# Opening feed-forwards and embedding gates with two tile pairs, chunk by chunk

## The chip, the cores and the metric

The kernel runs on one core of one Trainium2 chip. The metric is the device time of one execution in microseconds (us). Three runs of the kernel before took 1033.48, 1034.87 and 1036.57 us; their median, 1034.87, is the time before. In one more execution the hardware profiler took down every instruction.

## The reference

The program is a trunk of two layers over 256 positions of 1024 features. All weights and activations are float32.

```
for i in range(DEPTH):                                   # DEPTH = 2
    x = x + 0.5 * swiglu(rms_norm(x, norm_ffn1[i]), w_ffn1_gu[i], w_ffn1_down[i])
    h = rms_norm(x, norm_mix[i])
    mix = stick_breaking_attention(...) if i % 2 == 0 else multiscale_pool_mixer(...)
    x = x + mix
    x = x + 0.5 * swiglu(rms_norm(x, norm_ffn2[i]), w_ffn2_gu[i], w_ffn2_down[i])
    gate = sigmoid(rms_norm(x, norm_ple[i]) @ w_ple_gate[i])
    x = x + gate * (p[i] @ w_ple_proj[i])
```

`swiglu(h)` is `(silu(h @ w_gate) * (h @ w_up)) @ w_down` with an inner width of 2816. `rms_norm` divides by the root of the mean square over the 1024 features and multiplies by a gain.

## The kernel before, in words

**Layout.** x is held transposed: eight chunks of 128 features, each a tile of 128 partitions by 256 positions (`x[:, d]`). Every matmul multiplies a 128x128 tile of weights by a chunk, and sums over the chunks in a PSUM bank. A bank holds 512 columns, so two results of 256. Results rotate over six banks, three of the tag `z` and three of the tag `mm` (`next_bank`); two more, `st` and `o`, serve the statistics and attention.

**Splitting.** For accuracy each operand is split into a high part (rounded to the matmul's format) and a low part (the rest), and each product is three matmuls: high by high, high by low, low by high (`mm3`, lines 202 to 206; the matmul itself is line 130).

**Weights.** They come in 163 units of 128x2048 values, 16 tiles each, in the order of use. SyncE issues their loads. `divide` (lines 158 to 181) makes the high part (line 179 on ScalarE, or line 177 on VectorE) and the low part (line 181 on VectorE or GpSimd), in pieces. The table `SPLIT` gives for a unit (number of pieces, highs on VectorE, lows on GpSimd); the lows on GpSimd are the last ones. Units that aren't in it have (2, 0, 0). Raw values, highs and lows have three buffers each, so a unit's split can be written when the third unit before it is no longer read. `unit(u)` loads up to u + 3 and splits u and u + 1; `ahead` splits two units past the newest.

**Norm.** The gain goes into the chunks at once: line 268 makes the high part of a chunk on ScalarE, line 269 the low part on VectorE (tiles `xx`). The squares are made on the engine that `SQUARE` names (p GpSimd, a ScalarE, v VectorE, lines 280 to 282) and added up on GpSimd (line 283; the first square is line 273, the last sum is on VectorE). `statistics` (lines 293 to 326) adds them over the partitions with two matmuls into the bank `st` and makes r, the reciprocal root, with two ScalarE operations and four on VectorE (lines 288 to 291). r multiplies results after their matmuls, so matmuls needn't wait for it.

**Stages.** A feed-forward (`ffn`) has 22 tile pairs, one unit each, gate and up in one bank. Then 11 units for the way down: eight chunks of 22 tiles, each added to x (lines 400 to 403) and handed to the next norm at once. `project_late` begins a stage: the first unit takes the early chunks for both its results, and then the last ones (`LATE_FFN` says how many). `LEAD` says after how many pairs the statistics stand in TensorE's order; results wait in their banks till then. The embedding gate (`embed`) has four units and gives each result of 256 columns a bank of its own: lines 776 to 779 multiply by r, take the sigmoid (ScalarE), multiply by the projection and add to x, by way of a tile in SBUF, and then the next norm begins on that chunk. After the last layer the chunks are stored instead, and the last one goes in two halves.

**Units around the joints.** 49 is the embedding projection of layer 0, and 50 to 82 its second feed-forward (50 to 71 pairs, 72 to 82 the way down). 83 to 86 are the gates of layer 0. 87 to 119 are the first feed-forward of layer 1, 120 its embedding projection, 121 to 125 pooling. 126 to 158 are its second feed-forward, and 159 to 162 its gates.

**Order.** TensorE's and SyncE's instructions run in the order in which the program writes them (`manual_schedule`). A planner orders the other engines' when the program is built: what is ready goes first, by priority. `high_priority` blocks go ahead of the rest; otherwise what was written earlier goes first. Gates of the embedding, with the norm behind them, have high priority; splits and the feed-forwards' gates haven't. Engines wait for each other by semaphores that the planner places; two engines' accesses to one PSUM bank are kept apart by it.

Of the kernel before, what the change touches and what calls it, by code (L numbers as in the profile page):

```python
# [11 lines left out]
F32 = mybir.dt.float32  # L12
F32R = mybir.dt.float32r
AF = mybir.ActivationFunctionType
ALU = mybir.AluOpType

P = 128
D = 1024
S = 256
# [37 lines left out]

LATE_FFN = (1, 1, 2, 2)  # L60
LEAD = (2, 1, 2, 2)

# [3 lines left out]
    ("ffn1", 0): "aavvavpv",  # L66
    ("mixer", 0): "ppppapvp",
    ("ffn2", 0): "apppvavv",
    ("ple", 0): "paappppa",
    ("ffn1", 1): "ppvvpppv",  # L70
    ("mixer", 1): "aapppapp",
    ("ffn2", 1): "ppppapvv",
# [25 lines left out]
def trunk(ctx: ExitStack, tc: tile.TileContext, gxT, pT, wts, outT):  # L98
# [17 lines left out]
    def name(s):  # L116
        uid[0] += 1
        return f"{s}_{uid[0]}"
# [6 lines left out]
    def next_bank():  # L125
        turn[0] += 1
        return bank("z" if turn[0] % 2 else "mm")
# [65 lines left out]
    def ahead():  # L193

        divide(newest[0] + 2)
# [63 lines left out]
    def begin_norm():  # L259
        nonlocal xx, xh, xl, acc  # L260
        xx = act.tile([P, 2, NC, S], F32R, tag="xx", bufs=2, name=name("xx"))
        xh, xl = xx[:, 0], xx[:, 1]
        acc = tmp.tile([P, S], F32, tag="acc", name=name("acc"))
# [67 lines left out]
    def project(u, out, src, order=range(NC), halves=(0, 1), start=None, stop=None):  # L331

        start = order[0] if start is None else start
        stop = order[-1] if stop is None else stop
        two = isinstance(out, list)
        for i in halves:
            dst = out[i][:, :S] if two else out[:, i * S : (i + 1) * S]
            for k in order:
                mm3(
                    dst, tile_of(u, i * 8 + k), (src[0][:, k], src[1][:, k]),  # L340
                    (two or i == 0) and k == start, k == stop,
                )

    def project_late(u, out, src, order, late):

        a, b = order[: NC - late], order[NC - late :]
        project(u, out, src, a, start=order[0], stop=order[-1])
        project(u, out, src, b, start=order[0], stop=order[-1])


    def ffn(n, u0, order, last_norm, aside=None, before=None):
        late, lead = LATE_FFN[n], LEAD[n]
        with tc.tile_pool(name=name("ffn"), bufs=1) as pool:
            hx = pool.tile([P, 2, NFF, S], F32R, name=name("hx"))
            hh, hl = hx[:, 0], hx[:, 1]

            def gated(j, ps):
                s = tmp.tile([P, S], F32, tag="s", name=name("s"))
                nc.vector.tensor_mul(s, ps[:, :S], r)  # L359
                nc.scalar.activation(s, s, AF.Silu)  # L360
                nc.vector.tensor_mul(s, s, ps[:, S:])
                nc.scalar.activation(hh[:, j], s, AF.Copy)
                nc.vector.tensor_sub(hl[:, j], s, f(hh[:, j]))

            waiting = []
            for j in range(NFF):
                ps = next_bank()
                if u0 + j == 0:
                    for k in range(NC):
                        for i in range(2):  # L370
                            mm3(
                                ps[:, i * S : (i + 1) * S], tile_of(0, 2 * k + i),
                                (xh[:, k], xl[:, k]), i + k == 0, k == NC - 1,
                            )
                elif j == 0:
                    project_late(u0, ps, (xh, xl), order, late)
                else:
                    project(u0 + j, ps, (xh, xl))
                waiting.append((j, ps))
                if j == lead - 1:  # L380
                    if before is not None:
                        before()
                    statistics()
                if j >= lead - 1:
                    for w in waiting:
                        gated(*w)
                    waiting = []
                ahead()
                if j == 4 and aside is not None:
                    aside()  # L390
            r_ffn = r
            begin_norm()
            for d in range(NC):
                ps = next_bank()
                for k in range(NFF):
                    w = tile_of(u0 + NFF, d * NFF + k)
                    mm3(ps[:, :S], w, (hh[:, k], hl[:, k]), k == 0, k == NFF - 1)
                t = tmp.tile([P, S], F32, tag="s", name=name("s"))
                with tc.high_priority():
                    nc.vector.scalar_tensor_tensor(  # L400
                        out=t, in0=ps[:, :S], scalar=0.5, in1=r_ffn, op0=ALU.mult, op1=ALU.mult
                    )
                    nc.vector.tensor_add(x[:, d], x[:, d], t)  # L403
                    last_norm(d, d == 0)
        return u0 + UNITS_FFN
# [350 lines left out]
        return proj, some  # L756

    def embed(u0, proj, after):
        xs = (xh, xl)
        for i in range(4):  # L760
            banks = [next_bank(), next_bank()]
            if i == 0:
                project_late(u0, banks, xs, list(range(NC)), 1)
                statistics()
                if after is not None:
                    begin_norm()
            else:
                project(u0 + i, banks, xs)
            for half in range(2):
                d = 2 * i + half  # L770
                t = tmp.tile([P, S], F32, tag="s", name=name("gate"))
                with tc.high_priority():
                    src = banks[half][:, :S]
                    n = S // 2 if after is None and d == NC - 1 else S
                    for c in (slice(i, i + n) for i in range(0, S, n)):
                        nc.vector.tensor_mul(t[:, c], src[:, c], r[:, c])
                        nc.scalar.activation(t[:, c], t[:, c], AF.Sigmoid)
                        nc.vector.tensor_mul(t[:, c], t[:, c], proj[:, d, c])  # L778
                        nc.vector.tensor_add(x[:, d, c], x[:, d, c], t[:, c])  # L779
                    if after is not None:  # L780
                        after(d, d == 0)
                if after is None:
                    nc.sync.dma_start(outT[:, d], x[:, d])
            ahead()
        return u0 + 4


# [142 lines left out]
```

## Time and profile before

| | |
|---|---|
| median of three runs | 1034.87 us (1033.48 to 1036.57) |
| the profiled execution | 1035.21 us, its span 1033.5 |
| TensorE (PE) busy | 985.5 us, 7942 matmuls, mean granted clock 0.975 |
| VectorE (DVE) busy | 708.4 us |
| ScalarE (ACT) busy | 532.1 us |
| GpSimd (POOL) busy | 297.2 us |

A row of the timeline gives start, duration, engine, line, operation, tiles written and read, and in brackets how long the engine was idle before and what ended it. A row of a group gives the count, the busy time, the mean of one in ns, and the idle time ahead with what ended it. A row of stretches gives for each engine the busy time and, in brackets, the instructions, then the granted clock of TensorE, the DMA share and GB/s. A row of waits gives the total, how many and the longest. A row of the chain gives start and duration of a piece of the chain that ended last.

### The profile page before, as it was taken

How to read it: one execution, taken by the hardware profiler on the slowest of the kernel's cores; microseconds unless marked ns; L12 is line 12 of the kernel's file. 1: busy time of each engine (PE TensorE's matmuls, PEld its weight loads, DVE VectorE, ACT ScalarE, POOL GpSimd, SP SyncE). 2: the span in 40 equal slices, each digit the busy share in tenths (PEclk: the TensorE clock that was granted, in tenths of full speed). 3: DMA queues.
4: the chain of work that ended last, by engine and by line, in shares of the span. 5: the costliest groups of instructions: out<-in, count | busy, mean ns of one | idle time of the engine just before them, and what ended most of it. 6: DMA issues, size and time to landing. Idle time of an engine off the chain costs nothing.

```text
span 1033.5 us, 19057 instructions
## 1 busy us (share of the span) xinstructions
PE 985.5 (95%) x7942; PEld 967.8 (94%) x7942; DVE 708.4 (69%) x1021; ACT 532.1 (51%) x875; POOL 297.2 (29%) x294
## 2 busy tenths in 40 slices
PE   8999999998788899999999799999998799999998
PEld 8999999987787899999999799999988699999997
DVE  7865655588998855665668776565568966565666
ACT  5654444557686655454446455444352565454443
POOL 4300003746574540000166510000256510000253
PEclk8999999998898999999999899999999899999999
DMA  7655454453221265455553455545443265555541
GB/s 246 258 201 183 185 200 168 164 175 151 82 82 42 87 241 204 167 201 181 190 194 130 163 189 188 191 177 205 166 161 123 94 235 201 176 192 196 174 161 42
DMA packets 26727, 174.81 MB, mean 169 GB/s; under 512 B 2960, under 2 KB 4496, under 8 KB 6032
## 3 DMA queue, kind: packets, MB, share of 16 engines
q1 hardware_dynamic: 26640, 173.59, 46.7%
q8 instruction: 62, 1.02, 0.4%
q14 instruction: 25, 0.20, 0.1%
HBM read 172.53 MB, written 1.05 MB: 168 GB/s over the span
## 4 chain that ended last, share of the span: by engine, by line
PE 82%; DVE 14%; ACT 2%; issue 1%; DMA 1%; SPq 0%; DVEq 0%; ACTq 0%
PE mm L130 41%; PE z L130 40%; DVE s L676 2%; DVE xx L269 2%; DVE wl L181 2%; DVE ql L510 1%; PE o L130 1%; DMA gx<-gxT 1%; DVE kl L506 1%; DVE gx L779 1%; DVE sql L442 0%; DVE gate L778 0%; DVE sph L435 0%; DVE qkt L488 0%; DVE sp L532 0%
## 5 line engine op out<-in xcount | busy, mean ns | idle before, releaser
L179 ACT ACTIVATE wh<-raw 128x1024 fp32r<-128x1024 f32 (+2 forms) x408 | 342.0, 867 | 296.5 <-PE mm L130 114.3
L181 DVE TENSOR_TENSOR wl<-raw,wh 128x1024 fp32r<-128x1024 f32 (+2 forms) x299 | 333.1, 1129 | 96.1 <-ACT wh L179 95.6
L130 PE MATMUL mm<-xx,wh 128*128 128x256 f32 x1856 | 335.5, 282 | 0.0
L130 PE MATMUL z<-xx,wh 128*128 128x256 f32 x1600 | 293.3, 284 | 10.9 <-DVE xx L269 7.4
L130 PEld LDWEIGHTS mm<-xx,wh 128*128 128x128 f32 x1856 | 287.5, 190 | 0.5
L130 PEld LDWEIGHTS z<-xx,wh 128*128 128x128 f32 x1600 | 249.5, 191 | 13.3 <-DVE xx L269 9.3
L130 PE MATMUL mm<-xx,wl 128*128 128x256 f32 x928 | 261.4, 282 | 0.1
L130 PE MATMUL z<-xx,wl 128*128 128x256 f32 x800 | 226.3, 283 | 1.9 <-DVE wl L181 1.9
L181 POOL TENSOR_TENSOR wl<-raw,wh 128x512 fp32r<-128x512 f32 (+1 forms) x120 | 189.4, 1599 | 121.5 <-ACT wh L179 114.5
L130 PEld LDWEIGHTS mm<-xx,wl 128*128 128x128 f32 x928 | 176.4, 190 | 0.8 <-POOL wl L181 0.8
L130 PEld LDWEIGHTS z<-xx,wl 128*128 128x128 f32 x800 | 153.0, 191 | 2.6 <-DVE wl L181 2.6
L273 POOL TENSOR_TENSOR acc<-gx 128x256 f32<-128x256 f32 x8 | 5.5, 684 | 433.7 <-DVE gx L403 428.1
L130 PE MATMUL mm<-hx,wh 128*128 128x256 f32 x704 | 123.9, 280 | 0.0
L130 PE MATMUL z<-hx,wh 128*128 128x256 f32 x704 | 123.9, 280 | 0.0
L130 PEld LDWEIGHTS mm<-hx,wh 128*128 128x128 f32 x704 | 107.1, 188 | 0.0
L130 PEld LDWEIGHTS z<-hx,wh 128*128 128x128 f32 x704 | 107.1, 188 | 0.0
L130 PE MATMUL z<-hx,wl 128*128 128x256 f32 x352 | 98.5, 280 | 0.0
L130 PE MATMUL mm<-hx,wl 128*128 128x256 f32 x352 | 98.5, 280 | 0.0
L268 ACT ACTIVATE xx<-gx 128x256 fp32r<-128x256 f32 x64 | 31.8, 505 | 73.7 <-DVE gx L403 55.2
L130 PEld LDWEIGHTS mm<-hx,wl 128*128 128x128 f32 x352 | 67.2, 191 | 0.0
L130 PEld LDWEIGHTS z<-hx,wl 128*128 128x128 f32 x352 | 67.2, 191 | 0.0
L359 DVE TENSOR_TENSOR s<-mm,r 128x256 f32<-128x256 f32 x44 | 18.6, 423 | 62.5 <-PE mm L130 62.5
(190 smaller groups left out, 1038.5 us busy)
## 6 DMA issues: line engine op xcount, KB each, us to landing
raw<-wts SPq DMA_DIRECT2D x161, 1024.0 KB, 4.8
raw<-wts SPq DMA_DIRECT2D x7, 256.0 KB, 6.6
outT<-gx SPq DMA_DIRECT2D x8, 128.0 KB, 2.2
gx<-gxT SPq DMA_DIRECT2D x3, 256.0 KB, 5.9
p<-pT SPq DMA_DIRECT2D x2, 256.0 KB, 2.7
raw<-wts SPq DMA_DIRECT2D x2, 128.0 KB, 2.9
gx<-gxT SPq DMA_DIRECT2D x1, 165.0 KB, 2.4
gx<-gxT SPq DMA_DIRECT2D x1, 128.0 KB, 3.4
```

The lines of the kernel that those rows point to most:

```text
L130: nc.tensor.matmul(out, lhsT, rhs, start=start, stop=stop, skip_group_check=True)
L179: nc.scalar.activation(h[:, c], raw[u][:, c], AF.Copy)
L181: eng.tensor_sub(lo[:, c], raw[u][:, c], f(h[:, c]))
L268: nc.scalar.activation(xh[:, d], x[:, d], AF.Copy, scale=gc)
L269: nc.vector.scalar_tensor_tensor(out=xl[:, d], in0=x[:, d], scalar=gc, in1=f(xh[:, d]), op0=ALU.mult, op1=ALU.subtract)
L273: nc.gpsimd.tensor_mul(acc, x[:, d], x[:, d])
L359: nc.vector.tensor_mul(s, ps[:, :S], r)
L506: (nc.gpsimd if K_LOW[j] == "p" else nc.vector).tensor_sub(kl, y[:, S:], f(kh))
L510: nc.vector.tensor_sub(ql[b, a], y[b, :S], f(q[b, a]))
L676: nc.vector.tensor_add(n[:, :, lo:], s[:, :, lo:], s[:, :, lo - reach : PAD + S - reach])
L779: nc.vector.tensor_add(x[:, d, c], x[:, d, c], t[:, c])
```

## The change

Three things change together. `project_open` replaces `project_late` in feed-forwards 1 to 3 and in both embedding gates: the first two units are computed together, chunk by chunk, so that each chunk is used for all four results before the next. `LEAD` is 3 there, so the statistics of a feed-forward follow the third pair. In the gates a unit now has one bank for both its results. The sigmoid and both multiplications are done in that bank, 512 columns at once (in the last unit 256, 128 and 128), and chunks are stored in pairs. Units 83 to 91 no longer have lows on GpSimd, and the squares of the gates of layer 0, but the first, are made on ScalarE.

```diff
-    53: (4, 0, 4), 55: (4, 0, 4), 80: (4, 0, 0), 81: (4, 1, 3), 82: (4, 0, 4), 83: (4, 2, 2),
-    84: (4, 0, 4), 85: (4, 0, 1), 86: (4, 0, 2), 87: (4, 0, 2), 88: (4, 0, 2), 89: (2, 0, 2),
-    90: (4, 0, 1), 91: (4, 0, 1), 117: (2, 0, 1), 119: (2, 0, 1), 120: (4, 0, 1),
+    53: (4, 0, 4), 55: (4, 0, 4), 80: (4, 0, 0), 81: (4, 1, 3), 82: (4, 0, 4), 83: (4, 1, 0),
+    84: (4, 1, 0), 85: (4, 0, 0), 86: (4, 0, 0), 87: (4, 0, 0), 88: (4, 0, 0), 89: (4, 0, 0),
+    90: (4, 0, 0), 91: (4, 0, 0), 117: (2, 0, 1), 119: (2, 0, 1), 120: (4, 0, 1),
...
-LATE_FFN = (1, 1, 2, 2)
-LEAD = (2, 1, 2, 2)
+OPEN_FFN = (0, 2, 2, 2)
+LEAD = (2, 3, 3, 3)
...
-    ("ple", 0): "paappppa",
+    ("ple", 0): "paaaaaaa",
...
+    def project_open(us, outs, src, order):
+
+        for k in order:
+            for u, out in zip(us, outs):
+                project(u, out, src, (k,), start=order[0], stop=order[-1])
...
             waiting = []
-            for j in range(NFF):
+            if opened:
+                waiting = [(j, next_bank()) for j in range(opened)]
+                project_open(
+                    [u0 + j for j in range(opened)], [ps for _, ps in waiting], (xh, xl), order
+                )
+            for j in range(opened, NFF):
...
-                elif j == 0:
-                    project_late(u0, ps, (xh, xl), order, late)
...
     def embed(u0, proj, after):
+
         xs = (xh, xl)
+        first = [next_bank(), next_bank()]
+        project_open([u0, u0 + 1], first, xs, list(range(NC)))
+        statistics()
+        if after is not None:
+            begin_norm()
+        half = S // 2
         for i in range(4):
-            banks = [next_bank(), next_bank()]
-            if i == 0:
-                project_late(u0, banks, xs, list(range(NC)), 1)
-                statistics()
-                if after is not None:
-                    begin_norm()
+            if i < 2:
+                ps = first[i]
             else:
-                project(u0 + i, banks, xs)
...
+                ps = next_bank()
+                project(u0 + i, ps, xs)
+
+            parts = [(0, 2, 0, S)]
+            if after is None and i == 3:
+                parts = [(0, 1, 0, S), (1, 1, 0, half), (1, 1, half, S)]
+            for a, n, t0, t1 in parts:
+                d = slice(2 * i + a, 2 * i + a + n)
+                c = ps.rearrange("p (a b) -> p a b", a=2)[:, a : a + n, t0:t1]
                 with tc.high_priority():
...
+                    nc.vector.tensor_mul(
+                        c, c, r[:, t0:t1].unsqueeze(1).to_broadcast([P, n, t1 - t0])
+                    )
+                    nc.scalar.activation(c, c, AF.Sigmoid)
+                    nc.vector.tensor_mul(c, c, proj[:, d, t0:t1])
+                    nc.vector.tensor_add(x[:, d, t0:t1], x[:, d, t0:t1], c)
                     if after is not None:
-                        after(d, d == 0)
-                if after is None:
+                        for e in range(d.start, d.stop):
+                            after(e, e == 0)
+                if after is None and t1 == S:
                     nc.sync.dma_start(outT[:, d], x[:, d])
-            ahead()
+            if i:
+                ahead()
         return u0 + 4
```

More of the change, by code (lines that the diff above doesn't have):

```diff
@@ L348, in project_late @@
         project(u, out, src, b, start=order[0], stop=order[-1])
+    def project_open(us, outs, src, order):
+        for k in order:
+            for u, out in zip(us, outs):
+                project(u, out, src, (k,), start=order[0], stop=order[-1])
     def ffn(n, u0, order, last_norm, aside=None, before=None):
-        late, lead = LATE_FFN[n], LEAD[n]
+        opened, lead = OPEN_FFN[n], LEAD[n]
         with tc.tile_pool(name=name("ffn"), bufs=1) as pool:
@@ L759, in embed @@
         xs = (xh, xl)
-        for i in range(4):
-            banks = [next_bank(), next_bank()]
-            if i == 0:
-                project_late(u0, banks, xs, list(range(NC)), 1)
-                statistics()
-                if after is not None:
-                    begin_norm()
-            else:
-                project(u0 + i, banks, xs)
-            for half in range(2):
-                d = 2 * i + half
-                t = tmp.tile([P, S], F32, tag="s", name=name("gate"))
-                with tc.high_priority():
[L773 to L779, printed above, removed]
+        first = [next_bank(), next_bank()]
```

## The prediction

> **What bounds the kernel now.** I read the page first (span, engines, the chain that ended last), then the chain in order of time, then busy time by stretches, then waits, groups and instructions in the stretches where TensorE is not full.
>
> ```profile
> span 1033.5 us, 19057 instructions
> PE 985.5 (95%) x7942; PEld 967.8 (94%) x7942; DVE 708.4 (69%) x1021; ACT 532.1 (51%) x875; POOL 297.2 (29%) x294
> PE 82%; DVE 14%; ACT 2%; issue 1%; DMA 1%; SPq 0%; DVEq 0%; ACTq 0%
> ...
> 371.66 5.65 PE z L130 x48
> ...
> 545.00:590.00 45.00, 38.26 (x281) 36.91 (x280) 38.45 (x56) 25.54 (x49) 27.32 (x23) 0.89 0.41 144
> 765.00:825.00 60.00, 48.06 (x357) 45.23 (x356) 51.47 (x60) 25.46 (x45) 37.71 (x31) 0.94 0.30 106
> ```
>
> The profiled execution took 1035.21 us: 1033.5 of span and 1.7 around it. It stands 0.3 above the median of the runs, 1034.87. TensorE sets the end: inside a feed-forward it gets through a tile pair (48 matmuls) in 5.65 us without a gap, 0.118 each, and nothing the change does there can move it. Time is lost only at joints. The change touches four: **A**, attention to the second feed-forward of layer 0 (at 360); **B**, gates of layer 0 to the first feed-forward of layer 1 (545 to 590); **C**, pooling to the second feed-forward of layer 1 (814 to 830); **D**, the gates of layer 1 and the end. Joint B is the dear one:
>
> ```profile
> PE z L130 <- DVE xx L269: 4.3, 3, 1.9
> PE z L130 <- ACT xx L268: 1.8, 1, 1.8
> ...
> 574.00:578.60 4.60, 4.60 (x23) 4.52 (x22) 4.08 (x7) 1.76 (x3) 3.03 (x4) 0.50 0.86 321
> ...
> 582.57 2.07 PE z L130 x8
> 584.64 6.30 PE mm L130 x48
> 590.94 0.24 PE st L130 x2
> ...
> L269 DVE SCALAR_TENSOR_TENSOR xx<-gx,xx 128x256 fp32r<-128x256 f32 x8 | 8.8, 1113 | 0.6 <-ACT xx L268 0.6
> L779 DVE TENSOR_TENSOR gx<-gx,gate 128x256 f32<-128x256 f32 x8 | 6.4, 824 | 0.0
> L776 DVE TENSOR_TENSOR gate<-z,r 128x256 f32<-128x256 f32 x4 | 1.7, 416 | 0.0
> L181 POOL TENSOR_TENSOR wl<-raw,wh 128x512 fp32r<-128x512 f32 x8 | 11.8, 1483 | 9.4 <-ACT wh L179 9.3
> L283 POOL TENSOR_TENSOR acc<-acc,sq 128x256 f32<-128x256 f32 x6 | 5.7, 944 | 1.5 <-ACT sq L280 1.3
> ```
>
> TensorE waits for the chunks of the normed input (L268, L269), which come out of the gates. It then runs at half clock: 23 matmuls in 4.60 us where 2.7 would do. The first pair ends at 584.64, and the second, with the sum of squares behind it, at 591.2. VectorE is late because instructions with both inputs in SBUF are held up while GpSimd runs: L779 takes 0.82 and L269 1.11, where L776, of the same size with one input in PSUM, stays at 0.42.
>
> **The change, part by part.** *Joint B.* Gates become 512 wide, in PSUM. Three VectorE operations per pair replace six, and none has two SBUF inputs. All lows of units 83 to 91 move from GpSimd to VectorE.
>
> ```profile
> 544.57 2.47 PE z L130 x21
> ...
> 551.90 0.69 DVE L181 TENSOR_TENSOR wl<-raw,wh 128x512 fp32r<-128x512 f32 x1 [0.30 <-ACT wh L179]
> ...
> 566.77 1.05 DVE L181 TENSOR_TENSOR wl<-raw,wh 128x512 fp32r<-128x512 f32 x1
> ...
> L669 DVE TENSOR_TENSOR u<-mm,r 128x512 f32<-128x512 f32 x2 | 1.4, 684 | 0.0
> L288 DVE TENSOR_TENSOR t<-r 128x256 f32<-128x256 f32 x1 | 0.4, 417 | 0.0
> L291 DVE TENSOR_TENSOR r<-r,t 128x256 f32<-128x256 f32 x1 | 1.4, 1398 | 0.0
> ...
> 359.33 4.97 DVE L181 TENSOR_TENSOR wl<-raw,wh 128x512 fp32r<-128x512 f32 x8
> ```
>
> The opening of units 83 and 84 runs from 544.5 for 96 matmuls, 11.3 us, to 555.8. Chunk 7, at hand by then, is covered; the 0.3 wait for the statistics goes too. But split weights have three buffers, and until 555.8 both units hold one each. So the splits of 86 and 87 start only then, when before 86's started 5.65 us earlier; unit 88's start when 85 is done, near 561.8. The reciprocal root also starts one pair later. From 555.8 VectorE owes: the root, four operations at 0.42 (L288; up to 1.40 where GpSimd holds one, L291), 1.7; four gates of three operations at 0.69 (L669, the nearest row for a wide operation out of PSUM; the third, an addition into SBUF, is not shown: 0.42 to 0.84 by L776 and twice that), 8.3; eight L269 at 0.42 (as L288, of their size) to 1.11, taken 0.5 since only the seven instructions of the sum of squares still run on GpSimd, 4.0; the last sum 0.4; twelve lows of 86, 87 and 88 at 0.62 (4.97 over 8), 7.4. Together 21.8, and about 2 for the blocks from GpSimd's sum (seven of 0.94, a third of it hit). That ends near 579.6. The four squares that move to ScalarE, 0.32 to 0.64 each by L777 at half their width (below), hide in its free time: it is busy 25.5 of the 45.
>
> Order matters. Gates and chunk operations have high priority, lows have not: in the profile no low runs on VectorE between 551.90 and 566.77. So the lows of 87 and 88 come last. TensorE, whose order is written out, asks for 88's third piece already with chunk 0. It stops there till about 579, with 9 matmuls done and 87 to go: 10.2 us, to 589.3. The long stop costs clock, 1.6 to 1.9 (a stretch as in the row with 0.50). The end is near 591, where it was 591.2. **B: 0**. Its bounds are -11 (no stall: 555.8, the sums 0.4, two units of 5.65, the opening 11.3, so 578.9, and late chunks add 1 or so) and +3 (another low-priority delay of four lows).
>
> *Joint C.* Nothing is removed here. The opening asks for the second unit, 127, at once, with chunk 6: its pieces 1 and 3.
>
> ```profile
> 814.25 0.40 PE L130 MATMUL z<-xx,wh 128*128 128x256 f32 x2
> 816.87 0.95 DVE L177 CAST wh<-raw 128x512 fp32r<-128x512 f32 x1
> 819.29 1.12 DVE L181 TENSOR_TENSOR wl<-raw,wh 128x512 fp32r<-128x512 f32 x1
> 820.33 0.96 DVE L177 CAST wh<-raw 128x512 fp32r<-128x512 f32 x1
> 821.21 1.21 DVE L181 TENSOR_TENSOR wl<-raw,wh 128x512 fp32r<-128x512 f32 x1
> 823.14 1.28 DVE L181 TENSOR_TENSOR wl<-raw,wh 128x512 fp32r<-128x512 f32 x2
> ...
> 822.87 1.61 PE z L130 x11
> 824.48 5.53 PE mm L130 x47
> ```
>
> Unit 127 has two highs (L177) and four lows on VectorE: pieces 0 to 3 end at 820.4, 822.4, 823.8 and 824.4. VectorE has no gap in that stretch. Before, TensorE spent it on unit 126, three quarters covered, and turned to 127 at 824.3, when its pieces were just there; it was through at 830.0. Now it stops after 6 matmuls (815.0), does 3 at 822.4 and has 87 left at 824.4: 10.2 us, to 834.7. **That is +4.7.** Nine microseconds with three matmuls are longer than the low spell of joint B, so half clock is likely, at up to 1.9; I take 1.3. C: +6.0, bounds 4.7 and 8.
>
> The Trainium skill (TensorE: Matmul & The Clock Gate, Part 1) says that the clock halves after an idle window of about 3.4 us and comes back after a busy one; by it the stop at C would cost an estimated 1.7. The row at 574 shows 1.9 for 23 matmuls, and the sum goes by the rows.
>
> *Joint A.*
>
> ```profile
> 359.95 0.40 PE L130 MATMUL z<-xx,wh 128*128 128x256 f32 x2
> ```
>
> The eight lows at 359.33 (above) are piece 3 of unit 50, four of 51, three of 52. The opening reaches 51's piece 2 at 361.0, after nine matmuls from 359.95; it is done at 359.33 plus four times 0.62, 361.8. A: +0.8 (0 to 1.2). Later statistics (after three pairs, not one) cost nothing: six banks let TensorE run three pairs, 17 us, beyond them; the root (two operations on ScalarE, four on VectorE, none over 1.40) and nine gate operations at 0.42 take 12 at most.
>
> *Joint D.* The last gate now lies in one bank with its neighbour, and ScalarE works in that bank too.
>
> ```profile
> 338.10 0.38 ACT L569 ACTIVATE oh<-o 64x256 fp32r<-64x256 f32 x1 [0.48 <-DVE ol L570]
> ...
> 1016.04 1.40 DVE L291 TENSOR_TENSOR r<-r,t 128x256 f32<-128x256 f32 x1
> ...
> 1026.13 0.42 DVE L776 TENSOR_TENSOR gate<-z,r 128x256 f32<-128x256 f32 x1 [0.58 <-PE z L130]
> 1027.50 0.43 DVE L779 TENSOR_TENSOR gx<-gx,gate 128x256 f32<-128x256 f32 x1
> ...
> 1028.96 0.30 DVE gate L776
> 1029.26 0.02 issue
> 1029.29 0.32 ACT gate L777
> ```
>
> At L569 ScalarE, on the other rows and columns of a bank, waits for VectorE's read of the first half: two engines are kept apart by the bank. So nothing of the last tile starts before TensorE has left its bank, and its three parts go one behind the other: 1.8 for the first (1026.13 to 1027.93 before, then under the matmuls) and twice 1.3 for the halves (0.30, 0.32, 0.30, 0.30 and the hand-overs). That is 4.4 after the last matmul, where it was 1.6 (1028.96 to 1030.53): +2.8 (if parts overlapped after all, +1.2). The saved waits at the opening give back 0.4. The root, ready at 1017.44 before, comes a pair later less that, at 1022.7; three gates behind it, 6.2, end at 1028.9, and the matmuls at 1028.5: 0.1 to 0.4 more. D: +2.5, bounds 1.2 and 3.5. The stores, four of them merged in pairs, stay behind the same last addition.
>
> The Trainium skill (PSUM — Partial Sum Buffer, section on bank collisions) wants guards by bank and group of 32 partitions. That is finer than what L569 shows, whose rows lie in another such group; the two halves here share all rows, so the sum would be the same.
>
> Sum: 0.8 + 0 + 6.0 + 2.5 = +9.3. From 1035.2 that is 1044.5, and 0.3 less as a median: **1044.2**.
>
> **The rivals.** (1) *The planner draws the second unit's splits forward, because TensorE asks for them earlier.* One mechanism, at B and C: it decides if unit 88's third piece is done by 570 and 127's by 818. Then B gains 9 of its 11, C and A cost nothing, D stays: -6.5, **1028.4**. For it: VectorE orders are fixed ahead, and an order may follow TensorE's. Against it: lows waited 15 us at B (551.90 to 566.77) though TensorE wanted unit 87's at 567.6 (four units of 5.65 and the sums after 544.57). (2) *Only B comes free*, with blocks from GpSimd gone and lows slipped between gates, while C and D cost as forecast: -9 + 9.3 = **1035.2**, no change. For it: over 0.42 each, L269 and L779 alone lose 8 us there to GpSimd. Against it: the 21.8 that VectorE owes in a room of 12 before the opening. (3) *C alone does not stall*: 9.3 - 6.0, **1038.2**. Against it: nothing ahead of C changes. (4) *The sums on GpSimd keep blocking* L269 at 1.11, and lows fall behind by 4 more: **1048**.
>
> **How the numbers follow.** Forecast 0.54, rivals 0.17, 0.12, 0.11, 0.06. 0.3% is 3.1 us, about what runs spread over 1033.5 to 1036.6 can tell from no change. Faster 0.18, same 0.13, slower 0.69. The forecast's own range, from A to D's bounds with B between -4 and +3, is 1038 to 1049. The whole range, 1030 to 1049, takes in (2), (3) and (4) and leaves out most of (1).
>
> **What would show it.** B right: between 567 and 579 TensorE waits for VectorE's lows (L181) and not for L269, and no L779 is over 0.8. C right: a wait of some 7 us for L181 after six matmuls of the second feed-forward. D right: over 4 us of single-file gate operations after the last matmul. Wrong: the first pair of layer 1's feed-forward under way before 572 without a stop, or no wait for unit 127; either takes the sum to 1038 or below.

## The result, and the profile after

The changed kernel takes 1041.54 us, the median of its five runs, against 1035.42 for the kernel before, also of five, on the same chip. Four of the five lie between 1037.6 and 1042.19; the fifth, 1362.94 at a granted clock of 0.652, is not counted in the ratio. The ratio is 1.0051, with a 95% interval of 1.0026 to 1.0076: slower, by half a percent. The forecast was 1044.2. The profiled execution took 1041.04 us, 1039.3 of span and 1.7 around it, so it stands 5.8 above the profiled execution of before, where +9.3 was forecast.

The page of the changed kernel:

```profile
span 1039.3 us, 19004 instructions
PE 983.7 (95%) x7942; PEld 967.2 (93%) x7942; DVE 706.7 (68%) x1019; ACT 532.3 (51%) x874; POOL 268.8 (26%) x273
PE 83%; DVE 13%; ACT 2%; issue 1%; DMA 0%; POOL 0%; SPq 0%; DVEq 0%; ACTq 0%; POOLq 0%
```

The same 7942 matmuls run, TensorE sets the end as before, and GpSimd has 28 us less to do. The totals say nothing of where 5.8 us went. For that I measure each touched stretch from its first matmul in the timeline: **A** and **C** are the 22 pairs of a second feed-forward, up to the first matmul of its way down; **B** is the gates of layer 0 with the 22 pairs behind them; **D** runs from the first gate matmul of layer 1 to the end of the span.

| stretch | before | after | difference | forecast |
|---|---|---|---|---|
| A | 359.95 to 484.56: 124.61 | 358.10 to 483.18: 125.08 | +0.5 | +0.8 |
| B | 544.41 to 704.09: 159.68 | 545.36 to 701.86: 156.50 | -3.2 | 0 |
| C | 814.25 to 943.27: 129.02 | 812.22 to 946.89: 134.67 | +5.7 | +6.0 |
| D | 1005.45 to 1033.5: 28.05 | 1009.08 to 1039.3: 30.2 | +2.2 | +2.5 |

They add up to +5.1. The other 0.7 lies in stretches whose instructions are the same in both kernels, and the last section comes back to it. In the changed kernel L790, L793, L794 and L795 are a gate's four operations (times r, sigmoid, times the projection, added to x), which were L776 to L779.

**Joint A.** The waits of TensorE between 340 and 372, in the changed kernel:

```profile
PE z L130 <- DVE wl L181: 4.0, 2, 2.2
PE mm L130 <- DVE wl L181: 0.2, 1, 0.2
```

The second row is new (before has the first alone, 3.9): the opening reaches a low of unit 51 just before it is done.

**Joint B.** First the busy time of the same 45 us as before, then TensorE's waits between 545 and 592, then VectorE's timeline there:

```profile
545.00:590.00 45.00, 38.39 (x308) 37.78 (x307) 30.84 (x55) 26.70 (x51) 6.47 (x7) 0.92 0.38 139
```

```profile
PE mm L130 <- DVE wl L181: 3.9, 1, 3.9
PE z L130 <- DVE xx L269: 1.6, 1, 1.6
PE z L130 <- ACT xx L268: 1.1, 1, 1.1
```

```profile
556.76 2.62 DVE L181 TENSOR_TENSOR wl<-raw,wh 128x512 fp32r<-128x512 f32 x4 [6.51 <-ACT wh L179]
559.29 0.42 DVE L288 TENSOR_TENSOR t<-r 128x256 f32<-128x256 f32 x1
559.63 0.69 DVE L181 TENSOR_TENSOR wl<-raw,wh 128x512 fp32r<-128x512 f32 x1
...
562.31 0.68 DVE L181 TENSOR_TENSOR wl<-raw,wh 128x512 fp32r<-128x512 f32 x1
562.91 0.69 DVE L790 TENSOR_TENSOR z<-z,r 128x512 f32<-128x512 f32 x1
...
564.71 1.28 DVE L181 TENSOR_TENSOR wl<-raw,wh 128x512 fp32r<-128x512 f32 x2
...
571.30 0.68 DVE L795 TENSOR_TENSOR gx<-gx,mm 128x512 f32<-128x512 f32 x1
571.89 4.27 DVE L269 SCALAR_TENSOR_TENSOR xx<-gx,xx 128x256 fp32r<-128x256 f32 x7
576.09 4.16 DVE L181 TENSOR_TENSOR wl<-raw,wh 128x512 fp32r<-128x512 f32 x5
```

The count of matmuls is the quickest reading: 308 where there were 281, so 27 more at 0.118, which is the 3.2 us that B gained. TensorE still stops twice. It waits 2.7 us for the first chunk of the new norm, and then 3.9 us for the third piece of unit 88, whose lows stand behind seven L269. Two things are new. VectorE is idle for 6.5 us ahead of 556.76: units 83 and 84 hold two of the three buffers to the end of the opening, so there is nothing to split. And six of the eight lows of units 87 and 88 find room between the operations of the root and the gates; only the last two come late.

**Joint C.** TensorE's timeline (gaps in brackets, with what ended them), then its waits between 790 and 835:

```profile
812.96 0.28 PE L130 MATMUL z<-xx,wl 128*128 128x256 f32 x1
818.13 0.79 PE L130 MATMUL mm<-xx,wh 128*128 128x256 f32 x2 [4.89 <-DVE wh L177]
820.65 0.58 PE L130 MATMUL mm<-xx,wl 128*128 128x256 f32 x1 [1.73 <-DVE wl L181]
821.03 0.63 PE L130 MATMUL mm<-xx,wh 128*128 128x256 f32 x2
...
826.15 0.42 PE L130 MATMUL mm<-xx,wh 128*128 128x256 f32 x2
```

```profile
PE mm L130 <- DVE wh L177: 4.9, 1, 4.9
...
PE mm L130 <- DVE wl L181: 1.7, 1, 1.7
```

Before, TensorE waited at this place for the chunks instead (waits of the kernel before between 800 and 835):

```profile
PE z L130 <- DVE xx L269: 2.9, 4, 1.5
```

After six matmuls TensorE asks for unit 127. It gets the high of the first piece that it needs (the second of the four) 5 us later, and the low some 2 us after that: 6.6 us of waiting. It then runs at half clock (granted 0.50) to 826.15, 25 matmuls in 5.5 us where 2.95 would do. The waits of before, 2.9 us for L269, are gone in return. The Trainium skill (TensorE: Matmul & The Clock Gate, Part 1) has the clock come back after a busy window of about 3.4 us, and says that this window runs freely, so that the ramp varies. Joint B agrees with that length (granted clock 0.50 from 576.82 to 580.4, 3.6 us); C takes 5.5.

**The end.** The chain that ended last, in order of time (start, duration, what):

```profile
1027.97 4.14 PE mm L130 x35
...
1032.13 0.44 DVE mm L790
...
1032.60 0.38 ACT mm L793
...
1033.00 0.45 DVE mm L794
...
1033.47 0.43 DVE gx L795
...
1036.17 0.29 DVE gx L795
```

The three parts of the last unit go single file, first the tile of 256 columns and then the two halves, 4.4 us from 1032.11, all of it after the last matmul. Before, the first part ran under the matmuls, and 1.6 us were left.

### The profile page after: what moved, and what is told of

It reads as the page before. It is cut to its first block, busy times and chain, and to the rows that moved or that the text cites. A ratio compares the mean times of both kernels' runs of the same rounds, so it can differ in the third digit from the quotient of the medians.

```text
span 1039.3 us, 19004 instructions
## 1 busy us (share of the span) xinstructions
PE 983.7 (95%) x7942; PEld 967.2 (93%) x7942; DVE 706.7 (68%) x1019; ACT 532.3 (51%) x874; POOL 268.8 (26%) x273
## 4 chain that ended last, share of the span: by engine, by line
PE 83%; DVE 13%; ACT 2%; issue 1%; DMA 0%; POOL 0%; SPq 0%; DVEq 0%; ACTq 0%; POOLq 0%
PE z L130 41%; PE mm L130 41%; DVE s L685 2%; DVE wl L181 2%; DVE xx L269 2%; DVE ql L519 1%; PE o L130 1%; DVE kl L515 1%; DMA gx<-gxT 0%; DVE sql L451 0%; DVE sph L444 0%; DVE qkt L497 0%; DVE sp L541 0%; DVE s L692 0%; PE st L130 0%
## 5 line engine op out<-in xcount | busy, mean ns | idle before, releaser
L181 DVE TENSOR_TENSOR wl<-raw,wh 128x1024 fp32r<-128x1024 f32 (+2 forms) x318 | 346.2, 1107 | 121.6 <-ACT wh L179 120.7
L130 PE MATMUL mm<-xx,wh 128*128 128x256 f32 x1856 | 337.5, 282 | 4.9 <-DVE wh L177 4.9
L130 PE MATMUL z<-xx,wh 128*128 128x256 f32 x1600 | 293.2, 284 | 4.0 <-DVE xx L269 1.6
L130 PEld LDWEIGHTS mm<-xx,wh 128*128 128x128 f32 x1856 | 288.1, 191 | 5.6 <-DVE wh L177 5.1
L130 PE MATMUL mm<-xx,wl 128*128 128x256 f32 x928 | 262.3, 283 | 6.2 <-DVE wl L181 5.9
L130 PEld LDWEIGHTS z<-xx,wh 128*128 128x128 f32 x1600 | 250.3, 192 | 4.6 <-DVE xx L269 1.8
L130 PE MATMUL z<-xx,wl 128*128 128x256 f32 x800 | 226.5, 283 | 1.9 <-DVE wl L181 1.9
L181 POOL TENSOR_TENSOR wl<-raw,wh 128x512 fp32r<-128x512 f32 (+1 forms) x103 | 164.5, 1618 | 117.0 <-ACT wh L179 115.1
L130 PEld LDWEIGHTS mm<-xx,wl 128*128 128x128 f32 x928 | 176.6, 190 | 7.7 <-DVE wl L181 6.6
L130 PEld LDWEIGHTS z<-xx,wl 128*128 128x128 f32 x800 | 153.6, 192 | 2.1 <-DVE wl L181 2.1
L130 PE MATMUL z<-hx,wh 128*128 128x256 f32 x704 | 122.8, 279 | 0.0
L130 PE MATMUL mm<-hx,wh 128*128 128x256 f32 x704 | 122.8, 278 | 0.0
L130 PEld LDWEIGHTS z<-hx,wh 128*128 128x128 f32 x704 | 106.6, 188 | 0.0
L130 PEld LDWEIGHTS mm<-hx,wh 128*128 128x128 f32 x704 | 106.6, 188 | 0.0
L130 PE MATMUL z<-hx,wl 128*128 128x256 f32 x352 | 98.0, 278 | 0.0
L130 PE MATMUL mm<-hx,wl 128*128 128x256 f32 x352 | 98.0, 278 | 0.0
L130 PEld LDWEIGHTS mm<-hx,wl 128*128 128x128 f32 x352 | 66.8, 190 | 0.0
L130 PEld LDWEIGHTS z<-hx,wl 128*128 128x128 f32 x352 | 66.8, 190 | 0.0
L268 ACT ACTIVATE xx<-gx 128x256 fp32r<-128x256 f32 x64 | 31.4, 504 | 63.2 <-DVE gx L412 52.3
```

Source lines behind the costliest of these rows:

```text
L130: nc.tensor.matmul(out, lhsT, rhs, start=start, stop=stop, skip_group_check=True)
L181: eng.tensor_sub(lo[:, c], raw[u][:, c], f(h[:, c]))
L268: nc.scalar.activation(xh[:, d], x[:, d], AF.Copy, scale=gc)
```

## The experiments

The experiments have the changed kernel as their base, except where another one is named. Some lines are shifted there: L131, L182 and L270 are L130, L181 and L269. The kernel before was timed beside each group: 1035.12 for the first four, 1036.38 for the next four, 1035.83 for the last three. Each stage is measured in one profile. Where its code is the same in several runs, A opened takes 123.97 to 125.33 (five profiles) and not opened 124.60 to 124.62 (eight), B as changed 156.3 to 157.0 (five), C as before 127.8 to 129.0 (nine). The last 892 matmuls of B take 105.06 in all thirteen profiles, so what differs in B lies in its first 360.

| run | median us | ratio to before, 95% interval | B | C | D |
|---|---|---|---|---|---|
| c_late | 1034.26 | 0.9991 (0.9974 to 1.0007) | 156.32 | 129.03 | 30.5 |
| d_banks | 1037.85 | 1.0027 (1.0006 to 1.0048) | 157.01 | 134.57 | 28.6 |
| ffn_late | 1032.92 | 0.9981 (0.9966 to 0.9996) | 154.77 | 129.0 | 30.3 |
| best | 1031.61 | 0.9963 (0.9944 to 0.9981) | 154.35 | 129.03 | 28.6 |
| gpsimd_back | 1032.28 | 0.9963 (0.9939 to 0.9988) | 155.79 | 127.79 | 28.6 |
| sbuf_gates | 1031.09 | 0.9953 (0.9933 to 0.9973) | 157.36 | 127.79 | 29.4 |
| gates_late | 1027.52 | 0.9924 (0.9896 to 0.9952) | 150.24 | 128.99 | 28.3 |
| tables_only | 1024.27 | 0.9888 (0.9855 to 0.992) | 149.94 | 129.02 | 28.1 |
| root_later | 1024.86 | 0.9901 (0.9875 to 0.9926) | 151.20 | 128.99 | 28.25 |
| first127 | 1037.05 | 1.0011 (0.999 to 1.0032) | 156.40 | 132.01 | 30.2 |
| same_again | 1042.43 | 1.0061 (1.0028 to 1.0094) | 156.45 | 135.41 | 30.4 |

**c_late: joint C begun as before.** Of the feed-forwards only the last one goes back to `project_late`.

```diff
-OPEN_FFN = (0, 2, 2, 2)
-LEAD = (2, 3, 3, 3)
+LATE_FFN = (1, 1, 2, 2)
+OPEN_FFN = (0, 2, 2, 0)
+LEAD = (2, 3, 3, 2)
```

> The changed kernel, but the second feed-forward of layer 1 (joint C) begins as before: unit 126 first, its last two chunks late, statistics after two pairs. Theory (the opening at C waits for the splits of unit 127 and that is most of the loss): from the first matmul of this feed-forward to the first of its way down 129 us as before, where the changed kernel took 134.7; the time falls by 5.7, to 1036. Rival (the loss lies in the clock and in TensorE's pace elsewhere and only happened to fall there): the stage may move, the time stays near 1041.

C is back at 129.03, 5.6 less, and the time at that of the kernel before. The waits for unit 127 are gone, and before's own waits for the chunks have come back (waits of this kernel between 800 and 835):

```profile
PE z L131 <- DVE xx L270: 2.9, 4, 1.5
```

So the loss at C is the opening's. What its wait consists of is first127's question.

**d_banks: the last gate unit in two banks again.** Its parts are made by way of a tile in SBUF, still with the changed kernel's four operations (here L800, L803, L804 and L805).

```diff
+            elif after is None and i == 3:
+                banks = [next_bank(), next_bank()]
+                project(u0 + i, banks, xs)
...
+                if after is None and i == 3:
+                    src = banks[a][:, t0:t1].unsqueeze(1)
+                    if t0 == 0:
+                        t = tmp.tile([P, S], F32, tag="s", name=name("gate"))
+                    c = t[:, t0:t1].unsqueeze(1)
```

> The changed kernel, but the last gate unit of layer 1 has two banks again and its three parts go through a tile in SBUF. Theory (parts in one bank go one behind the other): the gate operations after the last matmul shrink from over 4 us to 1.6, the time falls by 2.2, to 1039.3. Rival (the tail is late because the statistics come a pair later): the parts still end 4 us after the last matmul, and the time stays near 1041.

D takes 28.6 instead of 30.2, and 5.85 us pass from the start of the last matmul to the end, where it was 7.50 (4.85 before). The single file is gone; a piece of the chain near its end, in order of time, shows what remains:

```profile
1029.22 0.58 DVE gx L805
1029.80 0.33 DVE gate L800
1030.14 0.59 DVE gx L805
1030.73 0.34 DVE gate L804
1031.07 0.93 DVE gx L805 x2
```

VectorE works without a gap through the gates that have waited for the later root, and the end comes 1.0 us later behind the last matmul than before.

**ffn_late: all feed-forwards begun as before**, the gates still opened.

```diff
-OPEN_FFN = (0, 2, 2, 2)
-LEAD = (2, 3, 3, 3)
+LATE_FFN = (1, 1, 2, 2)
+OPEN_FFN = (0, 0, 0, 0)
+LEAD = (2, 1, 2, 2)
```

> The changed kernel, but all feed-forwards begin as before (first unit with its last chunks late, statistics after 2, 1, 2 and 2 pairs); the gates still open with two pairs, in their banks, without GpSimd's splits. Theory (what B gains is GpSimd's absence, and the opening of the feed-forward there only makes TensorE ask for unit 88's splits too early): C gives back 5.7, A 0.5, and B gains 2 to 4 on top of the changed kernel's 3.2; 1031 to 1033. Rival (the opening of the feed-forward is what covers the late chunks at B): B gives its 3.2 back, and the time is near 1038.

C comes back, and B gains 1.7 more, a little less than expected. Without the opening the first pair doesn't ask for unit 88 at once, and the wait of 3.9 us for lows is gone. The waits for the chunks stay, and with them some of the stop.

**best: ffn_late and d_banks together.**

> Feed-forwards as before and the last gate unit in two banks as before; gates opened with two pairs, the others in their banks, no splits on GpSimd around joint B. Theory: the sum of the two runs before this one, 1029 to 1031, faster than both kernels by 0.4% or more. Rival (the costs overlap or the opening is needed at B): 1035 or more.

At 0.9963 it is faster than both kernels; the time is a little above the 1029 to 1031 that was expected. The next three runs take one part each out of it.

**gpsimd_back: the old tables in best.** The rows of `SPLIT` and of `SQUARE` are those of the kernel before.

```diff
-    53: (4, 0, 4), 55: (4, 0, 4), 80: (4, 0, 0), 81: (4, 1, 3), 82: (4, 0, 4), 83: (4, 1, 0),
-    84: (4, 1, 0), 85: (4, 0, 0), 86: (4, 0, 0), 87: (4, 0, 0), 88: (4, 0, 0), 89: (4, 0, 0),
-    90: (4, 0, 0), 91: (4, 0, 0), 117: (2, 0, 1), 119: (2, 0, 1), 120: (4, 0, 1),
+    53: (4, 0, 4), 55: (4, 0, 4), 80: (4, 0, 0), 81: (4, 1, 3), 82: (4, 0, 4), 83: (4, 2, 2),
+    84: (4, 0, 4), 85: (4, 0, 1), 86: (4, 0, 2), 87: (4, 0, 2), 88: (4, 0, 2), 89: (2, 0, 2),
+    90: (4, 0, 1), 91: (4, 0, 1), 117: (2, 0, 1), 119: (2, 0, 1), 120: (4, 0, 1),
...
-    ("ple", 0): "paaaaaaa",
+    ("ple", 0): "paappppa",
```

> The kernel of the run best with one part undone: units 83 to 91 have their lows on GpSimd again, and the squares of layer 0's gates are made where they were. Stage B, from the first matmul of layer 0's gates to the first of the next way down, took 159.7 us before, 156.5 changed, 154.4 in best. Theory (GpSimd's absence is what B gains): 158 or more, the time near 1035. Rival (gates with an operand in PSUM no longer mind GpSimd, and its help with the lows is worth as much as it holds up): 155 or less, the time near 1032.

B rises by 1.4 only, and the time doesn't move by what can be measured: my theory was wrong here. VectorE's groups between 545 and 591 show GpSimd's effect and its limits (count, busy time, mean in ns; L807 and L808 are the gates' last two operations):

```profile
L182 DVE TENSOR_TENSOR wl<-raw,wh 128x512 fp32r<-128x512 f32 x12 | 12.3, 1047 | 6.3 <-ACT wh L180 6.3
L270 DVE SCALAR_TENSOR_TENSOR xx<-gx,xx 128x256 fp32r<-128x256 f32 x9 | 8.7, 993 | 0.0
...
L807 DVE TENSOR_TENSOR z<-z,proj 128x512 f32<-128x512 f32 x2 | 1.4, 689 | 0.0
...
L808 DVE TENSOR_TENSOR gx<-gx,z 128x512 f32<-128x512 f32 x2 | 1.4, 678 | 0.0
```

The operations with two SBUF inputs are held up (L270 at 0.99), the gates in PSUM aren't: five of the twelve gate operations run while GpSimd is at work, and they take 0.67 to 0.69 like the others. The Trainium skill (SBUF — State Buffer, Who interferes with whom) says so: with one SBUF input at most, and outside the modes that use two ports, VectorE doesn't contend with GpSimd. What that is worth in time depends on the rest. Here VectorE idles 6.3 us ahead of the lows because buffers are held, and GpSimd takes many of the lows off it (12 of this size where the changed kernel has 25). No run has the old tables with wide gates and without the opening, so which of the two makes the tables worth so little here is not separated.

**sbuf_gates: best with gates 256 wide, in SBUF, a bank for each result**, opening kept (the loop of lines 771 to 779 of the kernel before).

```diff
-        first = [next_bank(), next_bank()]
+        first = [[next_bank(), next_bank()], [next_bank(), next_bank()]]
...
+                        nc.vector.tensor_mul(t[:, c], src[:, c], r[:, c])
+                        nc.scalar.activation(t[:, c], t[:, c], AF.Sigmoid)
+                        nc.vector.tensor_mul(t[:, c], t[:, c], proj[:, d, c])
+                        nc.vector.tensor_add(x[:, d, c], x[:, d, c], t[:, c])
```

> The kernel of the run best with one part undone: every gate has two banks and works through tiles in SBUF, 256 wide, as before the change; the opening of the gates and the splits without GpSimd stay. Theory (without GpSimd beside it VectorE does 256 in SBUF nearly as cheaply as 512 in PSUM): B 1 us longer, 155.5, the time near 1032.5. Rival (the bank is what frees the gates): B 157.5 or more, the time 1034.5 or more.

B takes 157.36, 3.0 more than best and between the two expectations; but this profile is of the slowest of the twelve runs (1038.08), and the median, 1031.1, is no higher than best's. That the gates in PSUM are worth something at B is not shown.

**gates_late: best without the opening of the gates.** The first unit takes chunk 7 late, the statistics follow it, as before.

```diff
-        project_open([u0, u0 + 1], first, xs, list(range(NC)))
-        statistics()
...
+                project_late(u0, ps, xs, list(range(NC)), 1)
+                statistics()
...
-            if i:
-                ahead()
+            ahead()
```

> The kernel of the run best with one part undone: the gates of both layers begin with one unit, its last chunk late, and the statistics after it; gates stay in their banks, splits without GpSimd. Theory (the opening of the gates covers only chunk 7, which made TensorE wait 0.3 us, and it makes the splits of units 86 and 87 wait for buffers, so it is worth nothing at B): B 153 to 155, the last stage 0.5 longer at its start and sooner with its root, the time within 1 of best. Rival (the opening is needed to cover chunk 7): B 157 or more, 1034 or more.

B falls by 4.1 to 150.24. I had taken the opening to be worth nothing; it costs 4 us.

**tables_only: the kernel before with the new tables alone.** The edit is that of gpsimd_back the other way round, and nothing else. The rows also move one high of unit 83 to ScalarE and one of unit 84 to VectorE, and cut unit 89 in four.

> The kernel before, with nothing changed but the two tables: no lows on GpSimd in units 83 to 91, and squares of layer 0's gates on ScalarE. Theory (GpSimd's absence is what B gains): B 155 to 157, the time 1031 to 1033, faster than before. Rival (the table alone overloads VectorE, and it is the narrow gates and the late first pair that cost): B 159 or more, the time 1035 or more.

This has the lowest ratio of all, 0.9888 (root_later's interval overlaps with its own), and B is 9.7 shorter: more than either expectation allowed. The median falls by 12.1; what it gains beyond B was not traced. The window of 45 us, and VectorE's groups there:

```profile
545.00:590.00 45.00, 43.40 (x363) 42.77 (x363) 38.86 (x80) 32.72 (x65) 5.68 (x7) 1.00 0.48 172
```

```profile
L181 DVE TENSOR_TENSOR wl<-raw,wh 128x512 fp32r<-128x512 f32 x28 | 19.0, 702 | 3.3 <-ACT wh L179 3.3
L269 DVE SCALAR_TENSOR_TENSOR xx<-gx,xx 128x256 fp32r<-128x256 f32 x9 | 4.6, 526 | 0.0
L779 DVE TENSOR_TENSOR gx<-gx,gate 128x256 f32<-128x256 f32 x8 | 4.3, 553 | 0.0
```

The lows on VectorE in the kernel before, in the same window:

```profile
L181 DVE TENSOR_TENSOR wl<-raw,wh 128x512 fp32r<-128x512 f32 x12 | 9.2, 792 | 1.8 <-ACT wh L179 1.8
```

363 matmuls where before had 281: 82 at 0.118 are the 9.7 us. VectorE makes more than twice the lows (28 for 12) and is hardly busier than before (38.86 for 38.45), since L269 falls from 1.04 to 0.53 and L779 from 0.82 to 0.55. TensorE waits 1.6 us in all, never long enough for the clock to drop (1.00).

**root_later: best with the first two gate units one after the other.** The statistics still stand behind the second.

```diff
-        project_open([u0, u0 + 1], first, xs, list(range(NC)))
+        project_late(u0, first[0], xs, list(range(NC)), 1)
+        project(u0 + 1, first[1], xs)
```

> The kernel of the run best, but the first two gate units run one after the other (the first with chunk 7 late) instead of chunk by chunk; the statistics still follow the second. Stage B took 154.4 us in best and 150.2 in gates_late, which has the statistics after the first unit. Theory (the opening costs 4 us because the root comes 5.65 later, and all gates with it): B 153.5 to 155, the time as best, about 1031. Rival (it costs because units 83 and 84 hold two of three weight buffers until 11.3 us are over, and the splits of 86 and 87 start too late): unit 83's buffer comes free early again, B 150 to 151.5, the time 1027 to 1028.

B is 151.20, as the rival expected, and the time, 1024.86, is lower than either expectation. So about three quarters of the opening's cost at B are gone, though the statistics stand where they do in best. The lows of unit 86 on VectorE, first in root_later, then in best:

```profile
552.03 2.50 DVE L182 TENSOR_TENSOR wl<-raw,wh 128x512 fp32r<-128x512 f32 x4 [1.56 <-ACT wh L180]
```

```profile
559.29 2.62 DVE L182 TENSOR_TENSOR wl<-raw,wh 128x512 fp32r<-128x512 f32 x4 [6.51 <-ACT wh L180]
```

They come 6.5 us after the stage's first matmul (545.58) where in best it is 11.4 (547.89), since unit 83 gives its buffer back after 48 matmuls. The opening costs mostly through the buffers that it holds; the 1.0 us that is left to gates_late may be the later root's. The same is to be seen at the end: root_later comes to within 0.2 of before in D (28.25), with the statistics behind the second unit. In best the root ends 17.0 us after the stage's first matmul, in root_later 14.9, mostly because the lows of unit 162, which the opening holds back, then run on GpSimd beside it (L292 takes 1.40 instead of 0.42).

**first127: the splits of unit 127 at high priority**, otherwise the changed kernel.

```diff
+FORWARD = (127,)
...
+        if u in FORWARD and u not in split:
+            with tc.high_priority():
+                return split_up(u, only)
+        return split_up(u, only)
```

> The changed kernel, but the splits of unit 127 have high priority when the planner orders VectorE and ScalarE; nothing else differs. Stage C, from the first matmul of layer 1's second feed-forward to the first of its way down, took 129.0 us before and 134.7 changed. Theory (C waits for those splits because they stand behind the chunks on VectorE): its six operations come before the last four chunks, the wait shrinks by 2 to 3, C 132 to 133, and the chunks, then late, keep the rest. Rival (the splits are late because their buffers are): nothing moves, C 134.7.

C falls by 2.7 to 132.01. TensorE's waits between 800 and 835:

```profile
PE mm L131 <- DVE wh L184: 2.7, 1, 2.7
PE mm L131 <- DVE wl L188: 1.8, 2, 1.6
```

L184 and L188 are L177 and L181 there. The wait for the highs falls from 4.9 to 2.7, so the order of VectorE's work was one part of it, as the theory said. TensorE still waits 4.5 in all: VectorE now makes the six splits one after another, from 813.10 to 818.28, and TensorE asks for the first of them at 812.

**same_again: the changed kernel once more**, with an empty line added and no instruction changed.

> The changed kernel once more, nothing edited. In the profile of before the way down of layer 0's second feed-forward took 59.9 us for 528 matmuls, in the changed one 62.2, and in layer 0's first it is the other way about. Theory (TensorE falls into one of two paces by chance, per stretch): some stretch of the same kernel takes the other pace. Rival (the pace belongs to the code): the same stretches take 59.9 and 62.2 as in its first profile.

It takes 1042.43, and B, C and D come out at 156.45, 135.41 and 30.4. The pace of TensorE in stretches without a wait differs from that of the first profile; the last section shows the rows.

## Why the prediction was right and where it was wrong

The direction held, and the time lies within the range (the bounds of the four terms add up to 1037 to 1051, where the text has 1038 to 1049; 1041.54 lies in both). Joints C and D were right in place, cause and near enough in size, A is too small to tell, and B was wrong. That the sum came within 2.7 us owes something to luck, since the zero at B stands for terms of up to 10 us, as the steps below show.

**A** (+0.8, measured +0.5). The new wait of 0.2 us stands where it was forecast. But the five profiles that open A lie from 0.6 below to 0.7 above the others, 0.2 above in the mean, so the +0.5 is not shown to be more than chance.

**C** (+6.0, measured +5.7). The second feed-forward stops after six matmuls, as the prediction said, for 6.6 us where "some 7" was given. One detail differs: most of the wait is for a high (L177), not for lows (L181). Two sizes were off and nearly cancel. TensorE went on for good 8.4 us after the stage's first matmul (820.65 less 812.22), where the sum has 10.2 (824.4 less 814.25): the stage began 1.2 us later beside VectorE's work, and the low that it needed was the third that VectorE made, with the last one right behind. And the half clock cost 2.6 where 1.3 was taken. c_late shows the opening to be the cause, and first127 that rival (1), splits drawn forward, would have been worth half of it at C; the planner didn't draw them forward by itself.

**D** (+2.5, measured +2.2). The chain after the last matmul took the 4.4 us that were worked out, and d_banks gives back 1.6 of D. The 0.1 to 0.4 for the later root didn't come: VectorE was idle for 0.47 us before the last unit's first part. With the single file gone the root does show, and root_later says why it is so late.

**B** (0, measured -3.2). The step that failed is the sum of VectorE's work, the 21.8 us and the 2 for blocks that were to hold TensorE "till about 579", 34.5 us after the first gate matmul (544.5). TensorE went on after 31.5 (576.82 less 545.36), and that is the miss; the half clock behind it cost 1.7, as forecast. In front of the low that TensorE waited for, the third piece of unit 88, stands all of that sum but the last low and the last addition, 22.8 us. VectorE did it in 20.0, from 556.76 to 576.8 without a gap. The gates' twelve operations took 7.4 where 8.3 was added up, since one of 0.69 starts 0.60 after the one before; the root's four took 1.2 for 1.7; and the eight L269, with GpSimd's blocks, 4.6 for 4.0 and 2. "So the lows of 87 and 88 come last" failed as well: the planner put four of them between the root's operations and two among the gates. That changed what TensorE waited for, 2.7 us for the first chunk (L268, L269) and then 3.9 for a low where one long wait for lows was forecast. It moved the end little, because the third piece of unit 88 still stood behind all gates and chunks. That no gate would be over 0.8 was right (0.68 to 0.70).

The zero also hid larger terms. The runs lead from before to after in steps, with B at each:

| step | B | difference |
|---|---|---|
| before | 159.68 | |
| the new tables alone (tables_only) | 149.94 | -9.7 |
| and gates wide, in their banks (gates_late) | 150.24 | +0.3 |
| and gates opened with two units (best) | 154.35 | +4.1 |
| and feed-forwards opened too (after) | 156.50 | +2.2 |

(gates_late and best also have the last gate unit in two banks, which lies in D.) The prediction had the means to see the first step. It said that L269 and L779 lose 8 us to GpSimd at this joint, and then let the removed blocks be eaten up by twelve lows that come late. That is not so without the opening, which keeps buffers back. gpsimd_back shows how much the order of the steps matters: with the gates wide and opened, the same tables are worth 1.4.

Rival (2), that B alone comes free, was right in sign but was given 9 us where 3.2 came. Rival (3), no stall at C, and (4), sums that keep blocking, fell: L269 took 0.63 in the mean and TensorE went on earlier, not later.

## What to carry to other kernels

Opening a stage with two units at once covers a late chunk, but it holds two weight buffers to the end of the opening (some 3 us at B by root_later) and asks for the second unit's splits at once: with three buffers count both before you count the cover. A joint with a change of several parts should be costed part by part, since one part can give back what another wins: here the new rows of two tables were worth 1.1% alone, and the three parts together lost 0.5%. Work on GpSimd is not free where VectorE is late and reads two operands from SBUF; moving it away paid here. Moving VectorE's operands to PSUM kept the gates from being held up, but no run shows it to make the kernel faster.

## What the runs showed of the hardware

TensorE has two paces at a full granted clock. In the four way-down stretches nothing waits, and the same matmuls run; here are 50 us of each in the changed kernel, and then of two of them in same_again, whose instructions are identical (the count of matmuls behind the first x is the pace):

```profile
140.00:190.00 50.00, 50.00 (x444) 50.00 (x443) 30.68 (x37) 21.98 (x29) 15.97 (x12) 1.00 0.51 183
490.00:540.00 50.00, 50.00 (x427) 50.00 (x426) 30.92 (x45) 20.54 (x32) 17.94 (x17) 1.00 0.52 182
710.00:760.00 50.00, 50.00 (x443) 50.00 (x442) 31.51 (x42) 21.84 (x29) 15.85 (x15) 1.00 0.52 190
950.00:1000.00 50.00, 50.00 (x426) 50.00 (x426) 28.83 (x37) 21.51 (x28) 13.36 (x13) 1.00 0.50 181
```

```profile
140.00:190.00 50.00, 50.00 (x427) 50.00 (x426) 28.90 (x36) 21.73 (x28) 15.94 (x12) 1.00 0.48 175
710.00:760.00 50.00, 50.00 (x427) 50.00 (x427) 30.52 (x40) 21.18 (x27) 13.40 (x13) 1.00 0.51 184
```

A stretch of 528 matmuls takes 59.73 or 62.06 us from its first start to its last, 4% apart: of the 52 such stretches in the thirteen profiles ten take the shorter time and the rest the longer, with nothing between. As an identical kernel shows another pattern, it isn't the code that chooses; what does stays open. One stretch weighs 2.3 us, 0.2% of the time, so single profiles can't be compared by their spans more closely than that. The profile of before has one quick stretch and that of after two, which gives after 2.3 us; against it stand 2.5 us more in layer 1's pooling, whose instructions are unchanged, and some 0.5 us that I haven't traced. I have no cause for the 2.5, but it isn't the change: between that way down and C the changed kernel took 50.5 us, and same_again 48.0, as before.
